# Another order of the four mixers in a hybrid block, and product banks for two of them

## The chip, the cores and the metric

One core of a Trainium2 chip runs the whole program. The metric is the device time of one execution in microseconds. Engines are named as in the profile: PE (TensorE matmul), PEld (its weight loads), DVE (VectorE), ACT (ScalarE), POOL (GpSimd), SP (SyncE, which here issues the DMAs).

## What is computed

A sequence of 256 tokens of width 1024 in fp32 goes through two layers of a first block and two layers of a second block. The change concerns the first block. Cut to what matters, one of its layers is:

```python
for l in range(DEPTH):                       # DEPTH = 2
    h = rms_norm(x, pre_mix_g[l])
    z = h @ w_in[l]                          # 1024 x 3256, split into the inputs of four mixers
    o_a = hgrn2_mixer(...)                   # first linear mixer: gated linear attention, keys of 64
    o_b = gla_mixer(...)                     # second linear mixer: the same recurrence, keys of 32
    o_c = mla_mixer(...)                     # softmax attention with low-rank queries and keys
    o_d = gdn_mixer(...)                     # gated delta rule, with short convolutions and a triangular solve
    mix = concatenate([o_a, o_b, o_c, o_d]) @ w_out[l]
    x = x + rms_norm(mix, post_mix_g[l])
    h = rms_norm(x, pre_ffn_g[l])
    x = x + rms_norm(conv_glu_ffn(h, ...), post_ffn_g[l])
```

The four mixers read the same h and are independent of each other, except that the second linear mixer's gate code is a 16-column piece of z that is computed with the delta mixer's columns.

## The kernel before

Every large product is three fp32r matmuls (high by high, high by low, low by high): `mm3` at lines 333 to 339. For this each weight block is loaded into a `raw` buffer by SP, copied into `wh` by ACT (L308) and its remainder into `wl` by DVE or POOL (L311). These blocks are the "units". They form one list in a fixed order (`plan_first`, L1237, walks the mixers in the order `PLAN1`), and only three ordinary `wh`/`wl` pairs exist (`WB = 3`), so the products follow the list with a lead of three units. A unit is used for both token tiles (rows 0 to 127 and 128 to 255) before its buffers come free.

PSUM has eight banks under four names with two banks each: `acc`, `pd`, `pc`, `pa`. Products take theirs from `self.acc()`, which walks through `acc, acc, pa, pa`, or from a name that is given (`first_banks`, `bank`). The small matmuls and transposes of a mixer take theirs from `self.pt()`, by the mixer's letter in `BANKS`: delta `pd`, attention `pc`, both linear mixers `pa`.

Each mixer is a Python generator in phases: `mixer_d` (L982) products, convolutions and preparation, then the triangular solve (with a round trip through DRAM at L1120, L1122, L1134 and L1144) and the outputs; `mixer_c` (L875) products and preparation, then attention; `mixer_a` (L758) and `mixer_b` (L817) products and gates, then `gla` (L675), the chunked scan, with eight levels for each mixer. `RUN1` gives the order in which the phases are written. Before, it is: delta products, second linear products, delta solve, first linear products, second linear scan, attention products, attention, first linear scan. The order written is a priority: a scheduler places the instructions of each engine at compile time by its own estimate of when operands, buffers and banks are there, and on the chip each engine then runs its list in order.

`mix_out` (L577) transposes a mixer's output, for each token tile, into `mTh`/`mTl` (L398, L400, L401). The output projection `big_out` (L520) takes eight units in the order `ORDER1`; units 0, 1 are the first linear mixer's, 2, 3 the second's, 4, 5 the attention's, 6, 7 the delta mixer's. It gathers the first token tile in two `acc` banks and the second in two `pc` banks. The first five units do both tiles each; the last three (`TAIL`) do all of the first tile, then all of the second. The norm behind it begins with the first tile (ACT L412).

Small tiles come from slots by letter (`SLOTS`): attention and second linear mixer share theirs, the first linear mixer has its own.

Of the kernel before, what the change touches and what calls it, by code (L numbers as in the profile page):

```python
# [11 lines left out]
F = mybir.dt.float32  # L12
# [14 lines left out]
NEG = -1e30  # L27
ORDER1 = (6, 7, 4, 5, 0, 1, 2, 3)
ORDER2 = (0, 1, 4, 5, 2, 3, 6, 7)
# [32 lines left out]
def host_constants():  # L62
# [23 lines left out]
    for s in LEVELS:  # L86
# [14 lines left out]
SLOTS = {"d": (("d0", 256, 4), ("d1", 1024, 8), ("d2", 2048, 10)),  # L101
# [4 lines left out]
SLOTS["m"] = SLOTS["d"]  # L106
SLOTS["e"] = (("c0", 256, 3), ("c1", 1024, 11), ("g2", 2048, 6))
# [4 lines left out]
GB = ("b", "b")  # L112
PLAN1 = ("d", "b", "a", "c")
RUN1 = (0, 1, 0, 2, 1, 3, 3, 2)
RUN2 = (0, 1, 0, 2, 1, 3, 0, 2, 3)
STAG = {"d": "d", "m": "d", "c": "c", "b": "c", "a": "a", "e": "e", "e2": "e"}

BANKS = {"m": ("pd", "pa"), "d": ("pd", "pd"), "c": ("pc", "pc"), "a": ("pa", "pa"), "b": ("pa", "pa"), "e": ("pa", "pa"), "e2": ("acc", "acc")}
NX = "N"
# [9 lines left out]
class K:  # L129
# [687 lines left out]
    def mixer_b(self, l, xT):  # L817
        nc, a = self.nc, self.a
        self.g = "b"
        p = self.fm(xT, ("bqk", l))  # L820
        q = self.z([128, 1, 256], "b_q")
# [3 lines left out]
        pc = self.pt()  # L825
        for t in range(2):
            nc.tensor.transpose(pc[:16, t * 128:t * 128 + 128], self.code[t], self.ident)
        code = self.z([16, 256], "b_code")
# [3 lines left out]
        bg = self.col_load(a["gla_b_gk"][l], 1, "b_bg")  # L832
# [4 lines left out]
        e = self.z([128, 256], "b_e")  # L837
# [5 lines left out]
        b = self.z([128, 1, 256], "b_b")  # L843
        nc.vector.tensor_tensor_scan(b[:, 0], self.c("scan"), x, 0.0, OP.mult, OP.add)
        pv = self.tm(xT, (("bg", l), 2, 512))
        v, g = [], []
# [28 lines left out]
    def mixer_c(self, l, xT):  # L875
        nc, a = self.nc, self.a
# [9 lines left out]
        for ap, o, n in ((a["mla_q_norm_g"][l], 0, 256), (a["mla_kv_norm_g"][l], 256, 128)):  # L886
            nc.sync.dma_start(gn[:, o:o + n], bass.AP(tensor=ap.tensor, offset=ap.offset, ap=[[0, 128], [1, n]]))
        pz = self.tm(xT, (("c", l), 2, 416))
        kT = [self.z([96, 2, 256], "c_kT") for _ in range(2)]
# [92 lines left out]
    def mixer_d(self, l, xT):  # L982
        nc, a = self.nc, self.a
        self.g = "d"
        pz = self.tm(xT, (("dz", l), 2, 280))
        code = [self.z([128, 16], "b_code", "b") for _ in range(2)]
        for t in range(2):
# [154 lines left out]
        for t in range(2):  # L1142
            V[t] = self.z([128, 4, 128], "d_V")
            nc.sync.dma_start(V[t], dense(self.scv, t))  # L1144
            p = four()
# [632 lines left out]
```

## Time and profile before

| | us |
|---|---|
| median of 3 runs | 1545.65 |
| lowest, highest | 1544.41, 1547.41 |
| the profiled execution | 1551.53 |
| its span | 1549.4 |
| PE busy in it | 1475.8 |
| DVE busy in it | 1002.3 |

The span runs from the first instruction to the last; the rest of the execution's time lies around it. The profile gives busy time of each engine, a clock that was granted to TensorE (1.00 is 2.4 GHz, 0.50 is 1.2 GHz), and for idle time what ended it. The mixing stage of layer 0 lies between about 10 and 201 us, that of layer 1 between about 400 and 600 us; the feed-forward parts and the second block fill the rest.

### The profile page before, as it was taken

Reading aid. Unit: us, or ns where it says so; the run is one execution under the profiler, and the core shown is the slowest. Engines: PE = TensorE matmul, PEld = TensorE weight load, DVE = VectorE, ACT = ScalarE, POOL = GpSimd, SP = SyncE. Lnnn points to the kernel's source line nnn. Section 1 sums busy time; section 2 is a strip of 40 time slices with the busy share of each in tenths; the row PEclk is TensorE's granted clock in tenths of the full one; section 3 lists DMA queues with packets and bytes.
Section 4 is the critical chain, followed back from the end, with each engine's and each line's share of the span. In section 5 each row is a group of like instructions: output and inputs, shape, how many; then the busy total and the mean of one; then the engine's idle time right before and its main releaser. Section 6 shows DMA issues by size and latency. Waiting matters only on the chain.

```text
span 1549.4 us, 24775 instructions
## 1 busy us (share of the span) xinstructions
PE 1475.8 (95%) x9491; PEld 1319.9 (85%) x9491; DVE 1002.3 (65%) x1741; ACT 825.3 (53%) x1435; POOL 280.1 (18%) x360
## 2 busy tenths in 40 slices
PE   7988999999998899999999999999999999999998
PEld 6967789999896787999978888899977888899996
DVE  5896667656698665656576875554566695654455
ACT  5634456545565344544555674555554575555553
POOL 1453320000244232000033122000015231100010
PEclk9997999999999789999999999999999999999999
DMA  7532155656453223566646343556554543465563
GB/s 233 152 109 84 55 160 182 190 183 199 140 157 112 77 71 110 182 186 190 184 142 192 104 139 116 179 188 190 190 184 135 166 124 110 130 190 186 189 195 109
DMA packets 165379, 236.80 MB, mean 153 GB/s; under 512 B 16052, under 2 KB 127246, under 8 KB 165262
## 3 DMA queue, kind: packets, MB, share of 16 engines
q1 hardware_dynamic: 165262, 235.24, 49.1%
q8 instruction: 74, 1.21, 0.3%
q14 instruction: 43, 0.35, 0.1%
HBM read 232.45 MB, written 2.76 MB: 152 GB/s over the span
## 4 chain that ended last, share of the span: by engine, by line
PE 79%; DVE 11%; ACT 4%; DMA 4%; issue 1%; POOL 1%; SPq 0%; ACTq 0%; DVEq 0%
PE acc L337 7%; PE acc L338 7%; PE acc L339 7%; PE pa L337 7%; PE pa L339 7%; PE pa L338 7%; PE pc L337 5%; PE pc L339 5%; PE pc L338 5%; PE pd L339 4%; PE pd L338 4%; PE pd L337 4%; DVE wl L311 2%; DVE gl_r L717 2%; ACT wh L308 1%
## 5 line engine op out<-in xcount | busy, mean ns | idle before, releaser
L311 DVE TENSOR_TENSOR wl<-raw,wh 128x1024 fp32r<-128x1024 f32 (+4 forms) x424 | 484.3, 1151 | 364.0 <-ACT wh L308 362.8
L308 ACT ACTIVATE wh<-raw 128x1024 fp32r<-128x1024 f32 (+4 forms) x420 | 433.1, 1035 | 410.3 <-PE pd L338 100.1
L311 POOL TENSOR_TENSOR wl<-raw,wh 128x1024 fp32r<-128x1024 f32 (+1 forms) x26 | 61.6, 2370 | 641.9 <-ACT wh L308 641.6
L339 PE MATMUL pa<-xTh,wl 128*128 128x256 f32 x512 | 145.6, 284 | 0.0
L337 PE MATMUL pa<-xTh,wh 128*128 128x256 f32 x512 | 145.5, 284 | 0.0
L338 PE MATMUL pa<-xTl,wh 128*128 128x256 f32 x512 | 145.1, 283 | 0.0
L339 PE MATMUL pd<-xTh,wl 128*128 128x256 f32 x432 | 122.4, 283 | 0.5 <-DVE wl L311 0.5
L337 PE MATMUL pd<-xTh,wh 128*128 128x256 f32 x432 | 122.3, 283 | 0.0
L338 PE MATMUL pd<-xTl,wh 128*128 128x256 f32 x432 | 122.2, 283 | 0.0
L337 PEld LDWEIGHTS pa<-xTh,wh 128*128 128x128 f32 x512 | 98.2, 192 | 0.3
L338 PEld LDWEIGHTS pa<-xTl,wh 128*128 128x128 f32 x512 | 98.2, 192 | 0.3
L339 PEld LDWEIGHTS pa<-xTh,wl 128*128 128x128 f32 x512 | 98.1, 192 | 0.2
L337 PEld LDWEIGHTS pd<-xTh,wh 128*128 128x128 f32 x432 | 82.8, 192 | 0.9
L338 PEld LDWEIGHTS pd<-xTl,wh 128*128 128x128 f32 x432 | 82.8, 192 | 0.9
L339 PEld LDWEIGHTS pd<-xTh,wl 128*128 128x128 f32 x432 | 82.8, 192 | 0.8 <-DVE wl L311 0.8
L338 PE MATMUL acc<-wl,f_h 128*128 128x512 f32 x200 | 78.4, 392 | 0.0
L338 PE MATMUL pc<-wl,f_h 128*128 128x512 f32 x200 | 77.8, 389 | 0.0
L339 PE MATMUL pc<-wh,f_l 128*128 128x512 f32 x200 | 77.5, 389 | 0.0
L339 PE MATMUL acc<-wh,f_l 128*128 128x512 f32 x200 | 77.2, 389 | 0.0
L337 PE MATMUL acc<-wh,xTh 128*128 128x512 f32 (+4 forms) x200 | 71.3, 360 | 1.4 <-ACT xTh L494 1.1
L337 PE MATMUL pc<-wh,f_h 128*128 128x512 f32 x200 | 71.3, 389 | 0.0
L337 PE MATMUL acc<-wh,f_h 128*128 128x512 f32 x200 | 71.3, 392 | 0.0
(635 smaller groups left out, 3815.5 us busy)
## 6 DMA issues: line engine op xcount, KB each, us to landing
raw<-in_w_in_dram SPq DMA_DIRECT2D x84, 512.0 KB, 3.8
raw<-in_w_mlp_up_dram SPq DMA_DIRECT2D x64, 512.0 KB, 3.7
raw<-in_w_mlp_down_dram SPq DMA_DIRECT2D x64, 512.0 KB, 3.5
raw<-in_ffn_w_gate_dram SPq DMA_DIRECT2D x44, 512.0 KB, 3.6
raw<-in_ffn_w_up_dram SPq DMA_DIRECT2D x44, 512.0 KB, 3.5
raw<-in_ffn_w_down_dram SPq DMA_DIRECT2D x44, 512.0 KB, 3.6
raw<-in_w_out_dram SPq DMA_DIRECT2D x32, 512.0 KB, 3.6
raw<-in_w_ple_gate_dram SPq DMA_DIRECT2D x16, 512.0 KB, 3.4
```

The lines of the kernel that those rows point to most:

```text
L308: nc.scalar.activation(h[:, p], raw[:, p], AF.Copy)
L311: e.tensor_tensor(l[:, p], raw[:, p], h[:, p].bitcast(F), OP.subtract)
L337: t.matmul(out, ah, bh, start=first, stop=False, skip_group_check=True)
L338: t.matmul(out, ah, bl, start=False, stop=False, skip_group_check=True)
L339: t.matmul(out, al, bh, start=False, stop=last, skip_group_check=True)
L717: nc.vector.tensor_tensor(R[:, j].rearrange("p h (b s) -> p h b s", s=s), ev[:, ft[j], :, 1][:, None].to_broadcast([128, 2, 128 // s, s]), ...
```

## The change

The mixers' products are planned in the order delta, attention, first linear, second linear; the phases are written in the order delta products, attention products, delta solve, first linear products, attention, first linear scan, second linear products, second linear scan. The output projection takes the attention's units first, then the first linear mixer's, the delta mixer's and the second linear mixer's. The attention's products and the second linear mixer's products are given `acc` banks by name; the second linear mixer's small matmuls ahead of its scan use `pc` instead of `pa` (its letter there is `b0`; the scan's stays `b`, on `pa`). The two gate code tiles, now read at the end of the stage, get buffers of their own. All of it holds for both layers of the first block.

```diff
-ORDER1 = (6, 7, 4, 5, 0, 1, 2, 3)
+ORDER1 = (4, 5, 0, 1, 6, 7, 2, 3)
...
+SLOTS["b0"] = SLOTS["b"]
...
-PLAN1 = ("d", "b", "a", "c")
-RUN1 = (0, 1, 0, 2, 1, 3, 3, 2)
+PLAN1 = ("d", "c", "a", "b")
+RUN1 = (0, 1, 0, 2, 1, 2, 3, 3)
...
-STAG = {"d": "d", "m": "d", "c": "c", "b": "c", "a": "a", "e": "e", "e2": "e"}
-
-BANKS = {"m": ("pd", "pa"), "d": ("pd", "pd"), "c": ("pc", "pc"), "a": ("pa", "pa"), "b": ("pa", "pa"), "e": ("pa", "pa"), "e2": ("acc", "acc")}
+STAG = {"d": "d", "m": "d", "c": "c", "b": "c", "b0": "c", "a": "a", "e": "e", "e2": "e"}
+
+BANKS = {"m": ("pd", "pa"), "d": ("pd", "pd"), "c": ("pc", "pc"), "a": ("pa", "pa"), "b": ("pa", "pa"), "b0": ("pc", "pc"), "e": ("pa", "pa"), "e2": ("acc", "acc")}
...
     def mixer_b(self, l, xT):
         nc, a = self.nc, self.a
-        self.g = "b"
-        p = self.fm(xT, ("bqk", l))
+        self.g = "b0"
+        p = self.fm(xT, ("bqk", l), self.bank("acc"))
...
-        pv = self.tm(xT, (("bg", l), 2, 512))
+        pv = self.tm(xT, (("bg", l), 2, 512), outs=self.first_banks("acc"))
...
-        pz = self.tm(xT, (("c", l), 2, 416))
+        pz = self.tm(xT, (("c", l), 2, 416), outs=self.first_banks("acc"))
...
-        code = [self.z([128, 16], "b_code", "b") for _ in range(2)]
+        code = [self.xp.tile([128, 16], F, name=f"code{t}", bufs=1) for t in range(2)]
```

## Rows read from the trace of the kernel before

**Rows 1.** The page: span, busy time, clock in 40 slices, chain

```profile
span 1549.4 us, 24775 instructions
PE 1475.8 (95%) x9491; PEld 1319.9 (85%) x9491; DVE 1002.3 (65%) x1741; ACT 825.3 (53%) x1435; POOL 280.1 (18%) x360
...
PEclk9997999999999789999999999999999999999999
...
PE 79%; DVE 11%; ACT 4%; DMA 4%; issue 1%; POOL 1%; SPq 0%; ACTq 0%; DVEq 0%
```

**Rows 2.** Windows: length, busy PE, PEld, DVE, ACT, POOL; clock, DMA

```profile
90.00:110.00 20.00, 16.27 (x89) 12.98 (x88) 18.88 (x52) 4.75 (x11) 9.07 (x15) 0.96 0.36 95
110.00:135.00 25.00, 17.61 (x89) 16.55 (x88) 12.60 (x29) 3.20 (x7) 3.81 (x9) 0.62 0.14 40
...
480.00:500.00 20.00, 13.08 (x69) 9.88 (x68) 19.60 (x50) 5.02 (x11) 10.73 (x20) 0.91 0.23 57
500.00:527.00 27.00, 20.01 (x101) 18.84 (x100) 14.90 (x37) 3.19 (x7) 4.61 (x9) 0.62 0.19 54
```

**Rows 3.** Timeline, PE, layer 0: start, us, line, out<-in, count, [idle]

```profile
96.51 0.34 PE L339 MATMUL acc<-wh,xTl 128*128 128x416 f32 x1
...
118.31 0.66 PE L398 MATMUL pa<-cf,hn_o 128*128 128x128 f32 x2 [4.86 <-DVE hn_o L592]
...
124.01 2.17 PE L1147 MATMUL pd<-cf,d_V 128*128 128x128 f32 x8 [1.73 <-DMA d_V<-scv]
...
129.28 0.63 PE L398 MATMUL pa<-cf,hn_o 128*128 128x128 f32 x2
129.56 0.69 PE L337 MATMUL pa<-wh,xTh 128*128 128x416 f32 x1
```

**Rows 4.** Timeline, PE: neighbouring products of 256, 512, 416 columns

```profile
43.13 0.61 PE L1045 MATMUL pd<-cf,d_lg 128*128 128x128 f32 x4
...
43.69 0.28 PE L338 MATMUL pa<-xTl,wh 128*128 128x256 f32 x1
43.81 0.28 PE L339 MATMUL pa<-xTh,wl 128*128 128x256 f32 x1
...
51.12 0.40 PE L337 MATMUL acc<-wh,xTh 128*128 128x512 f32 x1
51.36 0.39 PE L338 MATMUL acc<-wl,xTh 128*128 128x512 f32 x1
...
95.37 0.35 PE L339 MATMUL acc<-wh,xTl 128*128 128x416 f32 x1
95.56 0.35 PE L337 MATMUL acc<-wh,xTh 128*128 128x416 f32 x1
```

**Rows 5.** Timeline, DVE: last convolution reads of k and of v

```profile
44.54 1.90 DVE L1014 SCALAR_TENSOR_TENSOR d_c<-acc,d_cw,d_c 128x253 f32<-128x253 f32 x4
...
52.52 0.99 DVE L1014 SCALAR_TENSOR_TENSOR d_c<-acc,d_cw,d_c 128x254 f32<-128x254 f32 x2
```

**Rows 6.** Timeline, ACT and DVE: reads of the attention's first product

```profile
138.01 0.38 ACT L898 ACTIVATE c_sq<-acc 128x256 f32<-128x256 f32 x1 [0.65 <-PE acc L339]
...
140.25 0.34 DVE L905 SCALAR_TENSOR_TENSOR c_cn<-acc,rs,c_gn 128x128 f32<-128x128 f32 x1
```

**Rows 7.** Waits of SP's queue, 60 to 140 us: total us, times, longest

```profile
SPq L1134 <- DVE d_Y L1133: 7.7, 1, 7.7
...
SPq L1144 <- DMA scv<-d_Y: 1.9, 1, 1.9
```

**Rows 8.** Scans' first matmuls, last mixer output, projection's last product in the chain

```profile
L688 PE MATMUL pa<-gl_q,b_k x8: 377/379/483, 85.5 to 94.8; 128*128 128x256 f32 x8
...
L688 PE MATMUL pa<-gl_q,a_k x8: 377/379/382, 136.4 to 142.1; 128*128 128x256 f32 x8
...
L401 DVE TENSOR_TENSOR mTl<-pa,mTh x4: 422/424/426, 119.4 to 188.8; 128x256 fp32r<-128x256 f32 x4
...
201.30 0.24 PE acc L339
```

## The prediction

> **What bounds the kernel now.** I read four views in this order: the page, the windows of the two mixing stages, TensorE's timeline inside the worst stretch, and the queue waits of SyncE.
>
> The page says that TensorE carries the span: it is busy for 95% of 1549.4 us and holds 79% of the chain that ended last [rows 1]. So the question for any change of order is where TensorE idles or runs at a lower granted clock. The clock's row has three digits under 9: slice 4 (116 to 155 us) and slices 14 and 15 (504 to 581 us), inside the mixing stages of the two first-block layers [rows 1].
>
> The windows give the size. In layer 0, 90 to 135 us, TensorE is busy for 16.27 of 20 and 17.61 of 25 us: 11.1 us idle. Its granted clock is 0.96 and 0.62, a mean of the two levels 1.2 and 2.4 GHz, after the idle pieces. Busy time at a mean clock c does only c of its work, so 16.27 x 0.04 + 17.61 x 0.38 = 7.3 us more are lost. Layer 1, 480 to 527 us, shows the same hole: 13.9 us idle, and 13.08 x 0.09 + 20.01 x 0.38 = 8.8 us by the clock. Together the two holes cost 18.4 + 22.7 = 41.1 us [rows 2].
>
> The timeline says why TensorE had nothing to do. The attention mixer's products (416 columns) for the first token tile went into an acc bank and stopped at 96.51 us after three of four weight units. Those for the second token tile went into a pa bank, and their first one starts at 129.56, right behind the last output transpose (129.28) of the second linear mixer's scan, which keeps both pa banks turning until then. Three weight units were held all that time, so nothing later in the weight order could run either. In between TensorE has only the scan's and the delta solve's small pieces, waits 4.86 us for a head norm and 1.73 us for the solve's round trip through DRAM [rows 3]. That is bank sharing, not missing work.
>
> **The change part by part.** Each step below occurs in both layers.
>
> 1. The attention's products get both acc banks, and come second in the weight order. The wait for a pa bank behind a scan disappears; the 24 products that stood at 129.56 and later move to some 70 us earlier. Removed: the cause of the hole, not yet the hole.
>
> 2. The hole needs filler. Second in line before were the second linear mixer's products; they now come last and take the hole's place: 48 with 256 columns at 0.12 us and 48 with 512 at 0.23 to 0.24 us, from the distance of neighbouring starts [rows 4]. That is 5.8 + 11.3 = 17.1 us at full clock, against 11.1 and 13.9 us of idle time. The attention's own small matmuls, which no longer wait for late products, come on top. So I count the hole as filled and, with it, the clock as granted in full: -41.1 us. If the fill were placed too early by the scheduler, part of the hole would stay; the lower bound of the gain is then the half of it, 20 us; the upper bound is 46, with the clock loss of another 5 us that I see later in layer 1 only on the page's clock row and do not count.
>
> 3. New wait early. The acc banks are two, and when the attention's products come up they hold the delta mixer's k and v convolution inputs. Those are read by VectorE until 44.54 + 1.90 = 46.4 us (k) and 52.52 + 0.99 = 53.5 us (v) [rows 5]. TensorE is free for the next block at 43.13 + 0.61 - about 0.25 = 43.5 us [rows 4]. So the first token tile starts at 46.4 instead of 43.5: 2.9 us, less one group of the delta's broadcasts behind it (0.9 us, the same as the one in the row): 2.0 us. Three units give 18 products at 0.19 us [rows 4], 3.4 us, to 49.8; then the weight buffers are held and the second tile waits for v: 3.7 us idle. Catching up takes 18 + 12 products, 5.7 us, to 59.2. Then the first linear mixer's first products need an acc bank that the attention's norm has to finish reading: from first read to last this took 138.01 to 140.59 us, 2.6 us [rows 6], some of it beside the last products; 2 us remain. Sum 7.7, taken as 8 us a layer. Queued behind the waiting product is the whole weight stream; the delta mixer's transposes can still pass between. Bounds: 3 us (the convolutions pull ahead since VectorE has fewer other pieces) to 20 us (each of the three waits twice as long, and the clock falls on top).
>
> This is where a rule of the Trainium skill speaks against the change: Perfetto Trace Analysis, section Matmuls (under Optimizing Tensor Performance), asks that independent matmul groups rotate through different PSUM banks, so that the read-out of one overlaps the next group's products. Four product groups in a row on two acc banks do the opposite. By the rows the price is the 8 us above; taken strictly, by the rule, every hand-over would be exposed, which is the first rival below.
>
> 4. Queues. SyncE issues the weight loads in order with the solve's DRAM round trip: it stood 7.7 us for the solved block and 1.9 us for its return [rows 7]. Before, no load that TensorE needed stood behind these; now the six units of the second linear mixer do. Bounds 0 to 7.7 us a layer; I take 2, since the loads run three units ahead and the nearest row is the short wait. The five small loads of the attention move ahead of all this and cost nothing there, covered by the delta's products; the second linear mixer's gate loads move behind it, covered by the first linear scan. The code tile moved to its own buffer costs no instruction: 0.
>
> 5. The end of the stage. Before, both the attention and the first linear mixer ended at 188.8 + 0.4 = 189.2 us, and the output projection went on until 201.54, 12.8 us [rows 8]. Now the last pair of projection units belongs to the second linear mixer, and the other six can run in the acc and pc banks, since its scan turns in pa only. After its last tile TensorE has three units with 6 products for the first token tile, 18 x 0.23 = 4.1 us, before the norm starts. I count nothing for it: TensorE is busy there anyway in the row before, so this is only cover against a late end (second rival).
>
> Sum: -41.1 + 2 x 8 + 2 x 2 = -21.1 us. The profiled execution took 1551.53 us (span 1549.4): 1530.4. It lies 5.9 us over the median of the runs, 1545.65; so I expect a measured 1524.5 us.
>
> **The rivals.**
>
> A. The read-outs eat the gain. Each layer stalls 20 us early, so 41.1 - 40 - 4 is about -3: 1542 to 1549, no change at 1546. For it: two banks for four groups in a row, and VectorE is 94% busy in 90 to 110 [rows 2], so reads come late. Against it: the delta's broadcasts and transposes lie in the same stretch, and the three waits worked out from rows are short.
>
> B. Slower: the second linear scan stands at the very end and is late. Before, it ran from 85.5 to 129.9 us, 44 us, and the first linear scan from 136.4 to 189.2, 53 us [rows 3, 8]. If the two run one behind the other in VectorE, they take 97 us. With 4.1 us of projection left behind it, it must end by 201.5 - 4.1 = 197.4 to lose nothing, so the first linear scan must start by 100. Its inputs are there at about 93 by my count. If attention and solve hold it until 107, the end slips 7 us a layer, plus nothing gained: 1545.65 + 14, 1560 us. Against it: the two scans use different buffers for their large tiles, so they can overlap, and VectorE idles half of 110 to 135 [rows 2].
>
> C. The change doesn't do what it says: the scheduler places products by its own estimate; it may put the second linear products ahead of the hole, or leave the delta's tail as the last to end at the old time. Then the hole only moves: 1540 to 1548, at 1545.
>
> **How the numbers follow.** Forecast (holes filled, early stall about 8): 0.60 at 1524.5, with its own range 1505 (full 46 less an early stall of 3 a layer) to 1539. A 0.18, B 0.13, C 0.09. The range of 8 in 10 reaches into A and C: 1505 to 1547; above it lie B and a part of A, below it 0.05. A measurement of this kernel tells some 0.2%, 3 us, from no change. Faster: 0.60 + half of A + half of C, 0.74. Same: 0.11. Slower: 0.15.
>
> **What would show it.** In the profile after: no 416-column product in pa, and the attention's products from about 46 to 60 us with idle pieces of 2 to 4 us between, ended by VectorE's convolution or the attention's norm; the granted clock full where it is 0.62 now; 512-column products of the second linear mixer beside the solve at 95 to 125; the projection running before the last scan ends; the norm behind the projection starting near 190 us instead of 201.5, and each mixing stage 8 to 14 us shorter. The prediction fails if the early idle time is over 15 us a layer, if low-clock stretches appear in it, if the second linear scan's last tile comes after 197 us, or if the delta's last tile stays at 188 with TensorE idle before it.

## The result, and the profile after

The changed kernel takes 1558.89 us (median of 4 runs, 1558.49 to 1562.19) beside 1546.09 for the kernel before in the same series: ratio 1.0082, 95% interval 1.0054 to 1.0109, 12.8 us slower. The forecast was 1524.5 with a range up to 1547, so both the sign and the range were wrong.

The page of the profile after; its rows answer to [rows 1]:

```profile
span 1557.5 us, 24776 instructions
...
PE 1483.2 (95%) x9483; PEld 1318.5 (85%) x9491; DVE 1002.2 (64%) x1741; ACT 825.8 (53%) x1435; POOL 280.1 (18%) x360
...
PEclk9999899999989989999999999999999999999999
...
PE 77%; DVE 11%; DMA 5%; ACT 4%; issue 2%; POOL 1%; SPq 0%; ACTq 0%; DVEq 0%; POOLq 0%
```

Nothing in the page looks much different at first: the same work, nearly the same shares. The low digits of TensorE's clock (PEclk) have moved, from slices 4, 14 and 15 to slices 5, 12 and 15, and are a little less low (8 where 7 stood).

The windows view of the profile after, with the columns of [rows 2]: length, busy time of PE, PEld, DVE, ACT and POOL, granted clock, DMA. The second, third, seventh and eighth rows cover the windows of [rows 2]; the sixth is layer 1's stretch that corresponds to the first:

```profile
45.00:65.00 20.00, 15.38 (x86) 14.17 (x85) 16.85 (x37) 10.01 (x25) 8.58 (x16) 0.91 0.52 157
90.00:110.00 20.00, 19.84 (x119) 16.74 (x118) 18.66 (x47) 10.10 (x24) 9.91 (x14) 1.00 0.44 117
110.00:135.00 25.00, 22.58 (x166) 20.21 (x166) 20.35 (x44) 10.64 (x26) 12.94 (x20) 1.00 0.23 67
165.00:180.00 15.00, 9.61 (x59) 8.81 (x59) 13.06 (x30) 3.06 (x9) 8.08 (x11) 0.77 0.50 148
180.00:208.00 28.00, 25.67 (x132) 21.25 (x132) 13.23 (x30) 7.76 (x20) 6.67 (x11) 0.88 0.17 58
440.00:465.00 25.00, 21.51 (x113) 19.80 (x112) 17.91 (x44) 11.91 (x30) 11.50 (x22) 0.79 0.28 85
480.00:500.00 20.00, 20.00 (x110) 16.05 (x109) 13.56 (x35) 16.31 (x22) 4.63 (x9) 1.00 0.53 148
500.00:527.00 27.00, 23.91 (x158) 20.60 (x157) 25.60 (x52) 12.41 (x32) 17.81 (x21) 0.94 0.29 83
```

The old hole is filled. In 90 to 135 us TensorE idles 2.6 us at full clock, where idle time and clock cost 18.4; in 480 to 527 they cost 3.1 + 23.91 x 0.06 = 4.5 us instead of 22.7. That is 34 us of the 41.1 hoped for. But 45 to 65 now loses 4.6 + 15.38 x 0.09 = 6.0 us, and 165 to 208 loses 5.4 + 2.3 us idle and 2.2 + 3.1 by the clock, 13.0 us. There the kernel before lost 1.6 us:

```profile
165.00:180.00 15.00, 14.51 (x101) 12.50 (x100) 8.19 (x24) 6.63 (x23) 2.64 (x6) 1.00 0.35 106
180.00:208.00 28.00, 26.90 (x148) 22.09 (x146) 14.79 (x30) 11.15 (x22) 9.52 (x9) 1.00 0.39 127
```

One row for each whole mixing stage (from the first transposes of its norm to those of the next norm) gives the balance. Same columns, first two rows before, then two after:

```profile
9.60:207.98 198.38, 181.05 (x1179) 158.73 (x1179) 144.02 (x301) 100.93 (x211) 71.36 (x111) 0.94 0.43 130
400.30:605.90 205.60, 184.53 (x1181) 161.32 (x1180) 148.82 (x312) 105.47 (x220) 73.60 (x112) 0.92 0.37 111
```

```profile
9.38:207.72 198.34, 179.58 (x1177) 157.56 (x1179) 144.42 (x301) 100.23 (x211) 71.98 (x113) 0.95 0.43 131
402.18:609.56 207.38, 187.60 (x1179) 160.34 (x1181) 150.41 (x312) 105.28 (x217) 75.04 (x114) 0.93 0.35 106
```

The first number behind the window is the stage's length: 198.4 and 205.6 us before, 198.3 and 207.4 after. Length less busy TensorE is its idle time: 17.3 + 21.1 = 38.4 us before, 18.8 + 19.8 = 38.5 after. So the holes were not gained, they were moved. This does not hang on one pair of profiles: in the runs below that change only addresses, the same sum is 38.1 to 39.0 us in the old order (three runs) and 38.8 and 39.7 in the changed one. The lengths themselves are less sure, since each profile is one execution, and that of the kernel before took 1551.53 us, 5.4 more than its median: with those runs, the two stages together take 396.8 to 404.0 us in the old order and 398.2 to 405.7 in the changed one.

TensorE's timeline at the end of the stage of layer 0 (start, length, line, output and inputs, count, idle time before it; lines of the changed kernel stand one higher):

```profile
163.35 1.08 PE L728 MATMUL pa<-gl_r,gl_e 128*128 128x256 f32 x4
168.68 7.69 PE L736 MATMUL pa<-gl_r,gl_e 128*64 128x128 f32 x40 [4.24 <-DVE gl_r L718]
...
178.91 0.38 PE L399 MATMUL pd<-cf,hn_o 128*128 128x128 f32 x2
179.13 1.00 PE L1213 MATMUL pd<-d_vn,d_kd 128*128 128x64 f32 x8
...
198.76 0.38 PE L399 MATMUL pd<-cf,hn_o 128*128 128x128 f32 x2
200.06 0.50 PE L338 MATMUL pc<-wh,mTh 128*128 128x512 f32 x1 [0.92 <-ACT mTh L401]
...
201.09 0.38 PE L399 MATMUL pa<-cf,hn_o 128*128 128x128 f32 x2
```

The second linear scan (L728, L736) waits 4.24 us for VectorE, and the delta mixer's outputs (L399 in pd, L1213) stand behind it in TensorE's list until 178.9. That scan itself had started right behind the first linear mixer's last transpose:

```profile
155.75 0.38 PE L399 MATMUL pa<-cf,hn_o 128*128 128x128 f32 x2
155.97 1.03 PE L689 MATMUL pa<-gl_q,b_k 128*128 128x256 f32 x4
```

The last transposes come at 198.8 (delta) and 201.1 (second linear mixer), the low part of the last tile at 202.3; in [rows 8] the last low part came at 188.8.

The rest of the loss lies where no order was changed. Each of the four feed-forward parts (from the end of a mixing stage to the start of the next, or to the end of the program) is 1.0 to 2.1 us longer, 6.7 us in all, with the same instructions in the same order. There every product with f_h or f_l as its fixed operand starts later behind the one ahead of it than before. The first and last product of one feed-forward unit of 24, after:

```profile
999.79 0.39 PE L338 MATMUL acc<-wh,f_h 128*128 128x512 f32 x1
...
1005.13 0.40 PE L340 MATMUL pc<-wh,f_l 128*128 128x512 f32 x1
```

5.34 us for 23 steps, 232.3 ns each; all 26 units of the second block that stand by themselves show it, and in the kernel before all of them show 227.9. The program has 1296 of these products: 1296 x 4.4 ns = 5.7 us.

### The profile page after: what moved, and what is told of

It is laid out like the page before. It is cut to its first block, busy times and chain, and to the rows that moved or that the text cites. A ratio compares the mean times of both kernels' runs of the same rounds, so it can differ in the third digit from the quotient of the medians.

```text
span 1557.5 us, 24776 instructions
## 1 busy us (share of the span) xinstructions
PE 1483.2 (95%) x9483; PEld 1318.5 (85%) x9491; DVE 1002.2 (64%) x1741; ACT 825.8 (53%) x1435; POOL 280.1 (18%) x360
## 4 chain that ended last, share of the span: by engine, by line
PE 77%; DVE 11%; DMA 5%; ACT 4%; issue 2%; POOL 1%; SPq 0%; ACTq 0%; DVEq 0%; POOLq 0%
PE acc L338 7%; PE acc L340 7%; PE acc L339 7%; PE pa L339 6%; PE pa L338 6%; PE pa L340 6%; PE pc L340 5%; PE pc L338 5%; PE pc L339 5%; PE pd L340 4%; PE pd L338 4%; PE pd L339 4%; DVE wl L312 3%; DVE x L469 1%; PE pa L736 1%
## 5 line engine op out<-in xcount | busy, mean ns | idle before, releaser
L340 PE MATMUL pa<-xTh,wl 128*128 128x256 f32 x448 | 127.3, 284 | 0.0
L338 PE MATMUL pa<-xTh,wh 128*128 128x256 f32 x448 | 127.2, 284 | 0.0
L339 PE MATMUL pa<-xTl,wh 128*128 128x256 f32 x448 | 127.0, 283 | 0.0
L338 PEld LDWEIGHTS pa<-xTh,wh 128*128 128x128 f32 x448 | 86.0, 192 | 0.3
L339 PEld LDWEIGHTS pa<-xTl,wh 128*128 128x128 f32 x448 | 86.0, 192 | 0.4
L340 PEld LDWEIGHTS pa<-xTh,wl 128*128 128x128 f32 x448 | 86.0, 192 | 0.0
L338 PE MATMUL acc<-wh,xTh 128*128 128x512 f32 (+4 forms) x216 | 77.5, 365 | 3.3 <-DVE d_c L1015 2.0
L339 PE MATMUL acc<-wl,xTh 128*128 128x512 f32 (+4 forms) x216 | 77.2, 359 | 1.5 <-DVE wl L312 1.5
L340 PE MATMUL acc<-wh,xTl 128*128 128x512 f32 (+4 forms) x216 | 76.8, 357 | 0.8 <-DVE xTl L497 0.8
```

The lines of the kernel that those rows point to most:

```text
L338: t.matmul(out, ah, bh, start=first, stop=False, skip_group_check=True)
L339: t.matmul(out, ah, bl, start=False, stop=False, skip_group_check=True)
L340: t.matmul(out, al, bh, start=False, stop=last, skip_group_check=True)
```

## The experiments

Theory 1, formed from these traces: two things add up. The mixing stages are bound by a chain through VectorE, so that filling TensorE's hole only moves it; and the new code tiles shift all small tiles behind them by 128 bytes, which slows the feed-forward products. Its rivals: the prediction's own (TensorE bounds the stages, a PSUM bank makes the hole), and rival B of the prediction (the last scan's late start costs). Ratios are against the kernel before on the same chip.

| run | median us | ratio | interval |
|---|---|---|---|
| changed kernel, code tiles 128 B wide | 1552.53 | 1.0011 | 0.9990 to 1.0032 |
| before, code tiles as in the change | 1554.23 | 1.0043 | 1.0022 to 1.0065 |
| before, attention's products in acc | 1559.46 | 1.0059 | 1.0039 to 1.0079 |
| changed order without the bank edits | 1555.89 | 1.0037 | 1.0016 to 1.0059 |
| changed, second linear products earlier | 1559.44 | 1.0059 | 1.0037 to 1.0081 |
| changed, no GpSimd weight copies | 1549.63 | 1.0008 | 0.9993 to 1.0022 |
| changed, 5 of 8 scan levels left out | 1537.78 | 0.9923 | 0.9900 to 0.9946 |
| before, 5 of 8 scan levels left out | 1532.78 | 0.9892 | 0.9863 to 0.9921 |
| changed, without the low products | 1549.43 | 0.9984 | 0.9962 to 1.0005 |
| changed, without low products and low copies | 1525.40 | 0.9850 | 0.9822 to 0.9879 |
| changed, low copies away, all products kept | 1534.92 | 0.9908 | 0.9878 to 0.9937 |
| before, without the low products | 1542.17 | 0.9949 | 0.9931 to 0.9968 |
| changed, linear mixers exchanged | 1578.05 | 1.0195 | 1.0165 to 1.0225 |
| before, every second low copy on GpSimd | 1561.97 | 1.0078 | 1.0052 to 1.0104 |
| before, six copies a layer on ScalarE | 1551.65 | 1.0019 | 1.0001 to 1.0037 |

In all rows "changed" the code tiles are 128 bytes wide, so that the shift is 256 bytes. A difference of two rows is taken between their ratios, as a share of 1548 us; by the intervals it is uncertain by some 4 to 6 us.

### The shift of the small tiles

```diff
-        code = [self.xp.tile([128, 16], F, name=f"code{t}", bufs=1) for t in range(2)]
+        code = [self.xp.tile([128, 32], F, name=f"code{t}", bufs=1)[:, :16] for t in range(2)]
```

> The changed kernel with each of the two code tiles 128 bytes wide per partition instead of 64, so that every small tile behind them lies 256 bytes further than before the change instead of 128; no instruction differs. Address theory: the 512-column products whose stationary operand is f_h or f_l start every 231 to 232 ns in the changed kernel and every 227 ns before it, and it is the 128-byte shift of these tiles that does it; then they come back to 227 ns here, the four feed-forward stages lose about 6.5 us together, and the time is 1552 to 1553. Rival: the pace comes with the new order or with the run; then it stays at 231 and the time is 1557 to 1560.

and in the kernel before, the code tiles of the change alone:

```diff
-        code = [self.z([128, 16], "b_code", "b") for _ in range(2)]
+        code = [self.xp.tile([128, 16], F, name=f"code{t}", bufs=1) for t in range(2)]
```

> The kernel before with only the code tiles moved into buffers of their own, as the change does it: the 128-byte shift alone, with the old order, banks and instructions. Address theory: the feed-forward products whose stationary operand is f_h or f_l slow from 227 to 231 ns and the time rises by about 6.5 us, to 1552. Rival: no change, 1546.

Both came out as the address theory said: 1.0011 instead of 1.0082, and 1.0043 instead of 1. The same unit of 24 products as above in the changed kernel with 256 bytes:

```profile
990.65 0.40 PE L338 MATMUL acc<-wh,f_h 128*128 128x512 f32 x1
...
995.89 0.39 PE L340 MATMUL pc<-wh,f_l 128*128 128x512 f32 x1
```

5.24 us, 227.9 ns a step, with no instruction changed. The kernel before with the shift alone has 232.3. So the tile that "costs no instruction: 0" costs about 5.7 us by the paces, and 6.7 us (3.4 to 10) by the second run's ratio. What is left of the change, the order and the banks, is 1.0011: no difference that can be told.

Three more runs ask what the pace follows: with 96-byte tiles (192 bytes), one tile alone (64 bytes), and a constant tile ahead of everything 128 bytes longer, so that the streamed weights shift as well:

```diff
+        code = [self.xp.tile([128, 24], F, name=f"code{t}", bufs=1)[:, :16] for t in range(2)]
...
+        code = [self.xp.tile([128, 16], F, name="code0", bufs=1), self.z([128, 16], "b_code", "b")]
...
-        self.mhalf = self.cst.tile([128, 8], F, name="mhalf")
+        self.mhalf = self.cst.tile([128, 40], F, name="mhalf")
```

> The changed kernel with code tiles of 96 bytes: the small tiles lie 192 bytes further than before the change, no instruction differs. The products with f_h or f_l as stationary operand start every 227 ns at shifts of 0 and 256 bytes and every 232 at 128. If the address modulo 256 alone decides, 192 gives a third value between or the slow one; if it is a phase of 128 bytes, 192 reads as 64 and the value says on which side it falls; if the pace were the fast 227, only a shift by exactly 128 is slow.

> The kernel before with one code tile in a buffer of its own: the small tiles lie 64 bytes further. Shifts so far: 0 and 256 give 227 ns for products with f_h or f_l, 128 gives 232, 192 gives 229. If the pace falls off evenly on both sides, 64 gives 229 as well.

> The kernel before with one constant tile 128 bytes longer, so that all the weights' buffers, the activations and the small tiles lie 128 bytes further; no instruction differs but the length of one fill. If the distance between the streamed and the stationary operand decides, everything stays at 227 ns. If each address counts by itself, products with f_h and f_l are at 232 as in the run with the small tiles alone shifted, and those with xTh, xTl, mTh and mTl go from 227 to 232 too.

The paces by the same units: 228.7 to 229.2 ns at 192, 233.4 at 64, and 227.9 when both are shifted by 128:

```profile
989.11 0.40 PE L337 MATMUL acc<-wh,f_h 128*128 128x512 f32 x1
...
994.36 0.39 PE L339 MATMUL pc<-wh,f_l 128*128 128x512 f32 x1
```

(5.25 us.) So it is the distance between the fixed operand's address and the streamed one's, modulo 256 bytes in these five cases, and not either address. In the compiled program the first wh buffer lies at byte 36480 of a partition and the first f_h buffer at 195968 before the change, a multiple of 256 apart; after it f_h starts at 184064, which is 128 off. The run with both shifted has its f_h buffers at the very addresses of the run in the old order with the code tiles alone (196096 and on), and yet the other pace. The loss does not grow evenly to both sides: 64 is worse than 192.

### Is the hole a bank's?

```diff
-        pz = self.tm(xT, (("c", l), 2, 416))
+        pz = self.tm(xT, (("c", l), 2, 416), outs=self.first_banks("acc"))
```

> The kernel before with only the attention's products given both acc banks; order and all else as before. The prediction's reading (the wait for a pa bank at 96 to 130 us is the cause of the hole, and what is filled is gained): the hole of 18 to 23 us a layer goes without any new wait early, and the time is 1505 to 1525. Rival, from the trace of the changed kernel, in which idle and low-clock time only moved (27 us a layer in both): the hole closes or shrinks, but the last scan and the delta mixer's outputs end as late as before and the loss comes back ahead of them: 1538 to 1546.

The prediction's reading fails: the kernel is 9 us slower, and the hole stands. From 90 to 135 us it costs 11.5 us of idle time and 16.63 x 0.35 = 5.8 us by the clock, 17.4 beside 18.4 before:

```profile
90.00:110.00 20.00, 16.83 (x92) 14.42 (x92) 18.33 (x43) 7.00 (x11) 10.07 (x14) 1.00 0.53 161
110.00:135.00 25.00, 16.63 (x84) 16.08 (x85) 16.91 (x41) 6.18 (x18) 6.54 (x17) 0.65 0.39 121
```

TensorE's timeline, and below it VectorE's, in this run:

```profile
102.36 0.34 PE L339 MATMUL acc<-wh,xTl 128*128 128x416 f32 x1
102.63 3.07 PE L735 MATMUL pa<-gl_r,gl_e 128*64 128x128 f32 x24
...
123.08 0.66 PE L398 MATMUL pa<-cf,hn_o 128*128 128x128 f32 x2 [6.00 <-DVE hn_o L592]
...
138.14 0.50 PE L912 MATMUL pc<-cf,c_cn 128*128 128x128 f32 x3
```

```profile
133.65 0.48 DVE L904 SCALAR_TENSOR_TENSOR c_cn<-acc,rs,c_gn 128x256 f32<-128x256 f32 x1
```

All of the attention's products are complete by 102.7, 27 us before the second token tile's even began in [rows 3]. Their norm comes late all the same: ScalarE's first read of them (L898) starts at 129.42, and VectorE's step (L904) at 133.65. Both engines have it behind the solve and the second linear scan's head norms in their lists; VectorE is busy with these and with weight copies until 123, and then waits 1.97 and 2.29 us for ScalarE. The 24 products had not been held out of the hole; in the old order they are the last of the mixers' products, and behind them only the projection is left, which needs the mixers' outputs. They were the only filler near the hole, and now they stand ahead of it.

The bank edits of the change by themselves:

```diff
-        pz = self.tm(xT, (("c", l), 2, 416), outs=self.first_banks("acc"))
+        pz = self.tm(xT, (("c", l), 2, 416))
...
-        pv = self.tm(xT, (("bg", l), 2, 512), outs=self.first_banks("acc"))
+        pv = self.tm(xT, (("bg", l), 2, 512))
...
-        self.g = "b0"
-        p = self.fm(xT, ("bqk", l), self.bank("acc"))
+        self.g = "b"
+        p = self.fm(xT, ("bqk", l))
```

> The changed order without the three bank edits (attention's and second linear mixer's products take banks in turn from acc and pa, the second linear mixer's small matmuls use pa), code tiles 128 bytes wide. If the bank edits matter in this order, the attention's second token tile waits for a pa bank again and the time is 5 to 15 us above the run with the banks. If the order alone decides (in the new order no scan holds the pa banks when the attention's products come up), it is within 4 us of it, 1549 to 1556.

1.0037 beside 1.0011 for the same order with them: the intervals overlap. In this order the banks decide little.

### The late scan

```diff
-RUN1 = (0, 1, 0, 2, 1, 2, 3, 3)
+RUN1 = (0, 1, 0, 2, 1, 3, 2, 3)
```

> The changed kernel with 256-byte code tiles, and one thing more: the second linear mixer's product phase is written ahead of the first linear mixer's scan instead of behind it, so its products and gates have priority over that scan. In the changed kernel its scan starts at 155.97 us in layer 0, after an idle 13 us behind its last product, and its last tile comes at 202.3. Theory of the late scan: the end of the stage is set by when this scan may start; started 10 us earlier it ends some 10 us earlier, the idle and low-clock time behind 165 us (13 us a layer) falls by about half, and the time is 8 to 15 us below the run with the code tiles alone, 1538 to 1545. Rival, VectorE's total: the two scans and the solve share VectorE, so one scan's gain is the other's loss; within 4 us of that run, 1549 to 1557.

It is 7 us slower than the changed order alone (1.0059 beside 1.0011), and it does not test what it was meant to test. In layer 0 the second linear scan starts at 171.10 us, where it started at 154.41 with the changed order alone, and its last transpose comes at 206.30 beside 196.25:

```profile
171.10 1.03 PE L689 MATMUL pa<-gl_q,b_k 128*128 128x256 f32 x4
...
200.85 0.41 PE L399 MATMUL pa<-cf,hn_o 128*128 128x128 f32 x2 [1.58 <-DVE hn_o L593]
...
206.30 0.41 PE L399 MATMUL pa<-cf,hn_o 128*128 128x128 f32 x2 [0.49 <-DVE hn_o L593]
```

The first linear scan ends 17 us later (170.9 beside 154.2), and the second still begins right behind it. What the last scan's place costs was therefore not shown by starting it earlier; no run does that. Two more attempts at the end of the stage:

```diff
-POOLU = {'in': (0, 1, 3, 5), '2in': (0, 1, 3), 'ffn': (0, 1, 3), '2ffn': (0, 1, 3), 'ple': (0, 1), 'end': ()}
+POOLU = {'in': (0, 1, 3, 5), '2in': (0, 1, 3), 'ffn': (), '2ffn': (0, 1, 3), 'ple': (0, 1), 'end': ()}
```

> The changed kernel with 256-byte code tiles and without the low-part weight copies that GpSimd makes for the first feed-forward units behind each first-block mixing stage (VectorE makes them instead). In the changed kernel GpSimd works on two of these from 163.5 to 168.2 us, the scan's own GpSimd piece stands behind them, VectorE's six scan pieces beside them take 4.44 us instead of 2.5, and TensorE idles 4.24 us before the scan's products. Theory: these copies make that 4.2 us gap; it falls under 2 us, 2 to 3 us a layer, 5 us in all, below the run with the code tiles alone: 1546 to 1549. Rival: the gap is the scan's own chain or VectorE pays as much as GpSimd saved: 1550 to 1556.

1.0008, not to be told from 1.0011. The gap ahead of L736 goes from 4.2 to 3.0 us: GpSimd's copies make at most 1.2 us of it.

```diff
-PLAN1 = ("d", "c", "a", "b")
-RUN1 = (0, 1, 0, 2, 1, 2, 3, 3)
-ORDER1 = (4, 5, 0, 1, 6, 7, 2, 3)
+PLAN1 = ("d", "c", "b", "a")
+RUN1 = (0, 1, 0, 2, 1, 3, 2, 3)
+ORDER1 = (4, 5, 2, 3, 6, 7, 0, 1)
```

> The changed kernel with 256-byte code tiles and the two linear mixers exchanged: products in the order delta, attention, second linear, first linear; phases delta products, attention products, solve, second linear products, attention, first linear products, second linear scan, first linear scan; the projection takes attention, second linear, delta, first linear. If the order moves the loss but doesn't lessen it, as in the runs so far: within 6 us of the run with the code tiles alone, 1547 to 1559. If the place of the second linear scan is what costs, it stands beside the first linear mixer's products here and the time is 1535 to 1545.

Neither: 28 us slower than the changed order alone. The longer first linear scan is last here. An order can lose a lot; none of these won anything.

The same five scan levels taken out of both orders:

```diff
-        for lv, s in enumerate((128, 64) + LEVELS):
+        for lv, s in enumerate((128, 64) + (LEVELS if nft == 2 else LEVELS[:1])):
```

> The changed kernel with 256-byte code tiles and five of the eight levels of the second linear mixer's scan left out in both layers, so this mixer's output is not the reference's. A level is about 1.9 us of VectorE and 1.05 us of TensorE at full clock. Theory of the late scan: this scan stands alone at the end, so the five levels take 5 x 1.9 = 9.5 us a layer and some low-clock time off the end: 18 to 24 us below the run with the code tiles alone, 1529 to 1535. Rival, the end is set by something else (the delta mixer's last outputs, the weight stream): only TensorE's own 5 us a layer or less go, 1542 to 1550.

> The kernel before with the same five of eight levels of the second linear mixer's scan left out in both layers, so this mixer's output is not the reference's. Theory: in the old order this scan is the work in front of the hole at 97 to 129 us, VectorE runs it and the solve's 15 steps one behind the other, and the attention's norm (at 139.85, for a product that was complete at 97) stands behind both: the hole shrinks by 7 to 10 us a layer and the time by 14 to 22 us, to 1526 to 1534. Rival, the reading of the prediction (a bank that the scan's outputs hold): the same sign, since its outputs come earlier too; but if the hole is the solve's round trip alone, only TensorE's 5 us a layer or less go: 1538 to 1546.

13.6 us against the changed order alone (between the two expectations) and 16.7 against the kernel before. Within the intervals the scan costs as much in the middle as at the end, which speaks against its late place as what is dear.

### TensorE or VectorE?

The products by the weights' low parts leave TensorE in both orders (`MIX` names the mixers' weights, all but the delta mixer's first):

```diff
+MIX = ("dz", "dk", "dv", "aq", "af", "ag", "bqk", "bg", "c")
...
-    def mm3(self, out, a, b, first, last):
+    def mm3(self, out, a, b, first, last, skip=None):
...
-        t.matmul(out, ah, bl, start=False, stop=False, skip_group_check=True)
-        t.matmul(out, al, bh, start=False, stop=last, skip_group_check=True)
+        if skip != "b":
+            t.matmul(out, ah, bl, start=False, stop=last and skip == "a", skip_group_check=True)
+        if skip != "a":
+            t.matmul(out, al, bh, start=False, stop=last, skip_group_check=True)
```

> The changed kernel with 256-byte code tiles, and without the products by the low parts of the weights in the first block's mixers (all but the delta mixer's first 256 columns), so the mixers' inputs are less exact; the low parts are still made. That takes 144 products a layer from TensorE, some 22 us at the measured paces (80 of 256 columns at 0.12 us, 32 of 512 at 0.227, 16 of 416 at 0.19, 16 of 280 at 0.13), and nothing from VectorE. If TensorE's work bounds the mixing stages, the time falls by 40 to 44 us, to 1505 to 1512. If a chain through VectorE bounds them (TensorE's idle time was 37 to 42 us for the two layers in every order so far), most of it turns into idle time: 0 to 15 us, 1537 to 1552.

> The kernel before without the products by the low parts of the weights in the first block's mixers (all but the delta mixer's first 256 columns), so the mixers' inputs are less exact; the low parts are still made. TensorE loses some 22 us a layer, VectorE nothing. The prediction's reading (TensorE carries the span, the hole is a bank's): the time falls by 30 to 44 us, to 1505 to 1519. VectorE's chain as the bound, as in the changed order, where the same cut brought 3 to 5 us of 44: 0 to 10 us, 1539 to 1549.

Of 44 us of TensorE (144 products a layer, some 22 us by their paces), 4 came back as time in the changed order and 8 in the old one. The stage rows of the run in the changed order (columns as above), and below them those of the changed order alone:

```profile
9.82:211.67 201.85, 172.62 (x1035) 148.13 (x1035) 147.06 (x301) 99.73 (x211) 72.01 (x113) 0.88 0.43 128
406.47:606.46 199.99, 169.65 (x1036) 144.72 (x1037) 147.74 (x312) 106.32 (x218) 72.46 (x114) 0.89 0.38 111
```

```profile
9.77:202.86 193.09, 175.18 (x1177) 154.50 (x1178) 143.28 (x301) 100.30 (x211) 71.54 (x113) 0.97 0.44 134
396.16:601.29 205.13, 184.22 (x1178) 157.35 (x1180) 150.27 (x312) 105.06 (x216) 75.01 (x114) 0.95 0.36 107
```

Idle time is 29.2 + 30.3 = 59.6 us. In the run with the code tiles alone the same sum is 17.9 + 20.9 = 38.8, so 21 us became idle time; the granted clock fell to 0.88 and 0.89, which costs 172.62 x 0.12 + 169.65 x 0.11 = 39.4 us instead of 14.5 (175.18 x 0.03 + 184.22 x 0.05). 21 + 25 = 46: all that was taken away is lost again in these two ways. The split is rough, since the first profile is of an execution 7 us above its median and the second of one 6 below. The idle part is the surer one: in the old order the same cut raises the sum from 38.4 to 62.4 us, by 24. So about half of the removed work turned into waiting; the other half went with a lower granted clock, which is TensorE's own time.

Then VectorE's copies go too, and, in a third run, the copies alone, with every product kept:

```diff
-        for p in self.pieces(tot, PSPL if pool else DSPL if near else 1):
+        for p in [slice(0, 8)] if key[0] in MIX else self.pieces(tot, PSPL if pool else DSPL if near else 1):
...
+        l = h if key[0] in MIX else l
```

(the last line in the third run only)

> The same, and the low parts of these weights are not made either (8 columns of each unit are, so that the instruction stays): the mixers' inputs are less exact, and VectorE loses some 22 copies of 1.0 to 1.2 us, about 25 us a layer, beside the 22 us that TensorE lost. If VectorE's amount of work bounds the stages, this is 20 to 50 us below the run that still makes them; if it is the chain's own latency (each small step waits for the one before), or the weights' loads, it is within 8 us of it.

> The changed kernel with 256-byte code tiles, in which the low parts of the weights of the first block's mixers (all but the delta mixer's first 256 columns) are not made (8 columns of each are) and their products use the high parts a second time, so that TensorE has all its products and the mixers' inputs are not the reference's. If VectorE's chain alone bounds the mixing stages, this is as short as the run without these products: 1522 to 1532. If TensorE's 22 us a layer become the bound as soon as VectorE is lighter: about 1540 to 1550. Between these, both count in part.

Without both: 0.9850, 21 us below the run without the products. Without the copies alone: 0.9908, 16 us below the changed order alone, and its stage rows:

```profile
9.49:194.98 185.49, 176.95 (x1179) 154.88 (x1179) 124.91 (x297) 100.37 (x211) 60.38 (x113) 0.97 0.45 140
389.57:588.16 198.59, 182.10 (x1180) 156.55 (x1181) 124.72 (x312) 104.82 (x216) 68.70 (x114) 0.95 0.36 109
```

VectorE is busy for 125 us a layer instead of 143 and 150, TensorE has its full count of instructions (1179 and 1180), and its idle time falls to 8.5 + 16.5 = 25 us. So 44 us were taken from VectorE as well (46 in the run without both). TensorE's 44 us are worth 4 while VectorE is loaded and 9 when it isn't, which can't be told apart; VectorE's 44 us are worth 16, and its 46 are worth 21. Neither engine gives back its full 44. One rival is that TensorE waited for these copies as operands and not for VectorE's chain: with the changed order alone it waits 0.2 us for them in layer 0 and 3.1 in layer 1, of 38.8 us idle, so that is a small part at most.

Two runs try to use that without leaving anything out:

```diff
-        pool = i in self.npool
+        pool = i in self.npool or (key[0] in POOLK and key[-1] % 2 == 1)
```

(`POOLK`: the delta mixer's k and v and all products of the other three mixers)

> The kernel before with every second unit's low part in the mixers (delta's k and v, both linear mixers', the attention's) made by GpSimd instead of VectorE: 12 copies a layer, some 13 us of VectorE, become some 2.4 us each on GpSimd, which is busy for 18% of the span. If VectorE's amount of work bounds the stages, the time falls by 8 to 20 us, to 1529 to 1541. If VectorE stands still while GpSimd copies, or the copies come later than the products need them: within 6 us or slower, 1545 to 1560.

12 us slower. VectorE by groups in layer 0 of this run (line, output and inputs, form, count, busy time, mean ns of one):

```profile
L1074 DVE TENSOR_TENSOR d_kb<-d_qk,d_beta 128x256 f32<-128x256 f32 x2 | 3.8, 1880 | 0.1
L842 DVE TENSOR_SCALAR b_x<-b_x 128x256 f32<-128x256 f32 x1 | 2.3, 2307 | 1.5 <-ACT b_e L839 1.5
...
L1049 DVE TENSOR_SCALAR d_L<-pd,d_b 128x128 f32<-128x128 f32 x8 | 2.1, 343 | 0.0
```

The first took 554 ns before, the second 285; the third, which reads PSUM, took 340 and has hardly changed. The second one stands inside a GpSimd copy:

```profile
56.25 2.41 POOL L312 TENSOR_TENSOR wl<-raw,wh 128x1024 fp32r<-128x1024 f32 x1 [0.25 <-ACT wh L309]
```

```profile
56.51 2.31 DVE L842 TENSOR_SCALAR b_x<-b_x 128x256 f32<-128x256 f32 x1 [1.47 <-ACT b_e L839]
```

It ends 0.16 us behind GpSimd's. VectorE's busy time in the two stages falls by 6 us only, from 292.8 to 286.5, although 22 copies of 1.15 us (the page's mean), 25 us, have left it. Most of what GpSimd takes over, VectorE waits out. That agrees with the Trainium skill, SBUF — State Buffer, section Who interferes with whom: the two engines share a port pair that one of them holds for a whole instruction.

```diff
-                nc.vector.tensor_copy(kT[hh][64:96, :, ts], pp[64:96, 3][:, None, :].to_broadcast([32, 2, 128]))
+                nc.scalar.activation(kT[hh][64:96, :, ts], pp[64:96, 3][:, None, :].to_broadcast([32, 2, 128]), AF.Copy)
...
-            nc.vector.tensor_copy(qt, pp[:96])
+            nc.scalar.activation(qt, pp[:96], AF.Copy)
```

> The kernel before with the attention's six plain copies from PSUM a layer (rotated keys, transposed queries) made by ScalarE instead of VectorE, some 2.9 us of VectorE a layer. If VectorE's amount of work sets the stages' length, the time falls by 3 to 6 us, to 1542 to 1546. If only its pieces in front of the hole count (the scan and the solve at 97 to 124 us; these copies come behind it, at 139 and later), nothing: within 2 us.

No gain: 1.0019, though VectorE's busy time in the two stages falls from 292.8 to 285.1 us (ScalarE has the work instead). So not every piece of VectorE's work counts; these copies lie behind the hole. No kernel that computes everything beat the kernel before.

## Why the prediction was wrong

**Opening, what bounds the kernel.** "TensorE carries the span" was read from 95% busy, a mean over the whole span. In the mixing stages it is 91 and 90% by the stage rows, and when 44 us of TensorE's work are taken out of these stages, the time falls by only 4 and 8 us. This is the step that failed: it made every filled microsecond a gained one, in step 2. "Bank sharing, not missing work" failed too: with the banks given and the old order, the hole stays at 17.4 us. The held weight units kept nothing out of it, since only the projection came behind them.

**Step 1** (the wait for a pa bank goes) was right: the attention's products stand in acc from 47.0 to 58.1 us, and none of 416 columns is in pa.

**Step 2** (the hole is filled, -41.1) was right as to the fill, -34, and wrong as to its worth. A filled hole is a gain only if the stage's end moves, and the idle time of the two stages stayed at 38.4 and 38.5 us. The fill was taken from the stage's end, which then stood empty.

**Step 3** (early wait, 8 us a layer) came out near in its sum, 6.0 us in layer 0 and 8.0 in layer 1 (440 to 465), and within its bounds, but partly by luck. The waits in layer 0 are 1.2 us for k (2.0 counted), 0.8 for v (3.7) and 2.7 for the attention's norm (2); the rest is the clock, 0.91 and 0.79, which the sum left out and which was named as a sign of failure. Rival A, whose condition was 20 us a layer, is out.

**Step 4** failed in its last sentence: the code tile was costed by its instructions, and its bytes cost 5.7 us elsewhere. SyncE's waits for the solve are 4.7 and 2.6 us, and in layer 0 TensorE waits for no weight behind them.

**Step 5** (nothing for the end) was mis-sized: 13.0 us in layer 0. (By its own figures, 201.54 less 189.2 is 12.3 us, not 12.8; nothing hangs on it.) The sign named for the last scan's last tile was there (202.3 us, 197 named), and the delta mixer's last transpose came at 198.8, later than the 188 that was named.

**Rivals.** B gave 1560, and part of its picture is there: the second linear scan starts where the first one ends, and its last tile is 4.9 us behind B's limit of 197.4. But B's condition, a first linear scan that is held until 107, was met only in layer 1, where that scan starts 97.7 us behind the stage's start, as late as that; in layer 0 it starts at 97.7, 88 us behind it. And neither stage slipped by B's 7 us (198.3 and 207.4 beside 198.4 and 205.6); 5.7 us of the loss are the addresses, which B did not have. So its number is near in part by luck. Cutting the second linear scan is worth no more at the end than in the old order; the scan's late start by itself was not tested. C ("the hole only moves", 1545) is the nearest to what the order does once the shift is undone, 1.0011, though the products did go where the change meant them to. It had a chance of 0.09.

**The sum as measured.** 12.8 us are 5.7 by the paces and 1.7 (between -1.5 and 5) for order and banks; about 5 us are left over. The intervals (8.4 to 16.9 us for the change, 4.2 to 10.7 for the two parts together) overlap, so these may be no more than scatter. The profiles offer one candidate: the clock cost in the mixing stages, from the stage rows, was 25.6 us before, 22.1 after and 14.5 with the tiles shifted back, in runs whose instruction order is the same for the last two. It varies too much from run to run to be given a cause here: in the runs that change only addresses it is 17.9 to 23.5 in the old order and 14.4 and 14.5 in the changed one.

**Open.** That VectorE's load counts for more in these stages than TensorE's is shown by what was taken away: 16 to 21 us beside 4 to 9, of 44 each. That it does so as one chain is argued, not shown. Which of its pieces are on such a chain, and how much is their own time and how much the waits between them, is not known; the attempt with ScalarE only shows six that bring nothing. Why the granted clock fell when TensorE's work was taken away was not tested either.

## What to carry to other kernels

Before filling a hole, take the would-be bound's work away (here a third of the mixers' products) and see whether the time moves; an engine that is busy for 95% of a span can still not bound the stage in question. When the order of independent work changes, add up the idle time over the whole stage, not over the hole. And when a small buffer is added, look whether every tile behind it has moved, and keep fixed and streamed operands of large products at the distance that was fast, here a multiple of 256 bytes.

## What the hardware showed that was not expected

The pace of a 512-column fp32r product depends on where its two operands lie to each other: 227.9 ns when the fixed operand's address differs from the streamed one's by a multiple of 256 bytes, 232.3 at 128 off, 233.4 at 64 and about 229.0 at 192. In the 26 units of the second block that stand by themselves it is the same to 0.1 ns within a run (to 0.5 at 192), and the same between the three runs at a multiple of 256 and the two at 128. The Trainium skill, TensorE: Matmul & The Clock Gate, section Step-by-step: what each phase is for, says that loading the next tile's weights takes no SBUF read bandwidth from the running matmul; here something between the two costs up to 5.5 ns a product, and the measurement decides. Whether it is their reading was not shown, only that their distance matters.
